# Attention scores of two heads: the products with the keys' low halves on 64 rows each, one head in the lower rows of TensorE, the other in the upper

## The chip, the cores and the metric

The kernel runs on one core of a Trainium2 chip, in one launch. The metric is device time in microseconds (us) from start to end of one execution; the median of several executions is compared. TensorE (PE) multiplies matrices, with its loads of the stationary operand shown apart (PEld); VectorE is DVE, ScalarE is ACT, GpSimd is POOL, and SyncE (SP) issues the transfers.

## What is computed

Two layers of a backbone over 512 latent tokens with a prefix of 256 context tokens, width 1024. Each layer projects its normed input once (`w_in`) to all branches: multi-scale pooling, windowed attention (8 query heads, 2 key/value heads, window of 128, all of the context, a sink per head) and differential attention (4 heads, each with two sets of scores over all 768 keys). The branches are gated, merged, and followed by a squared-ReLU MLP. The second layer needs no output for the context. What the change touches are the scores of the latent queries:

```python
s_loc = jnp.einsum('bnqhgd,bnkhd->bnhgqk', qb, kb, preferred_element_type=jnp.float32) * scale
s_ctx = jnp.einsum('bnqhgd,bkhd->bnhgqk', qb, k_ctx, preferred_element_type=jnp.float32) * scale
...
s1 = jnp.einsum('bqhd,bkhd->bhqk', q1, k1, preferred_element_type=jnp.float32) * scale
s2 = jnp.einsum('bqhd,bkhd->bhqk', q2, k2, preferred_element_type=jnp.float32) * scale
```

The head dimension is 64, half of TensorE's 128 rows.

## The kernel before

**Two halves.** Products run in float32r, a float32 of fewer bits. So that little is lost, each operand is split: a high half (rounded by ACT) and a low half (what is left, subtracted by DVE). A general product takes three matmuls: high by high, low by high, high by low. Each matmul has its own weight load.

**Scores.** With a head dimension of 64 the two halves of a query stand in one operand. `proj_tr` (L485) transposes the rotated queries of two heads into one PSUM tile and writes `Q`, 128 rows by head pair, head and 128 queries: for head 0 the high half lies in rows 0 to 63 and the low half in rows 64 to 127, for head 1 the other way round. The keys are transposed twice, so that rows 64 to 127 repeat rows 0 to 63, and split into `KH` and `KL`. One matmul of `Q` with `KH` over 128 rows so gives (high + low of the query) by the key's high half, and one of `Q` with `KL` adds the part with the key's low half, into the same PSUM tile `S`, two banks of 512 columns; there are two such tiles.

**Units.** A unit is 128 queries by two heads. `diff_unit` (differential, 16 units in each layer) takes 768 keys in pieces of 512 and 256 columns (L533, L534). `swa_unit` (windowed, 16 units in each layer) takes for the first and the last block of queries two pieces of 256, for the two in the middle pieces of 128, 384 and 128 (L698, L699). The stages of a unit are A (scores, row minimum on DVE at L535 or L700, exponential on ACT at L537 or L704), B (scaling), B2 (transposes `ptr` on PE, L557 or L737), C (product with the values), D. `diff_ctx` and `swa_ctx` handle context queries in the first layer and aren't changed.

**Order.** `attention` runs the units as a pipeline of steps: in each, B2 of the unit before, A of this one, and between them the projection of the next head group (`z`, L398) in two halves, its rotation and transposes, C and D of earlier units, and whole gate products (`gate`, L1016 to L1018) that have nothing to do with the scores. A scheduler then fixes each engine's order from priorities. PE executes in that fixed order.

After attention come the merge (`br`), `out` and the MLP (`ff`), nearly all matmuls of 256 or 512 columns.

Of the kernel before, what the change touches and what calls it, by code (L numbers as in the profile page):

```python
# [134 lines left out]
class Kern:  # L135
# [377 lines left out]
            d["Q"][t] = q  # L513


    def diff_unit(self, l, d, qt):
        nc = self.nc
        mm = nc.tensor.matmul
        KH, KL, V, hd = d["KH"], d["KL"], d["V"], d["gi"]
        u = {}  # L520
        kts = list(range(6)) if qt < 4 else [4, 5]
        ka = kts[0] * 128
        n = 768 - ka
        nk = len(kts)

        def A():
            q = d["Q"].pop(qt)
            u["nm"], u["r"], u["E"] = self.sm(2, "nm"), self.sm(2, "r"), []
            nm, r = u["nm"], u["r"]
            for i in range(2):  # L530
                S = self.s("S")
                for (c0, c1) in ((ka, 512), (512, 768)) if qt < 4 else ((512, 768),):
                    mm(S[:, c0 - ka:c1 - ka], q[:, 0, i, :], KH[:, i, c0:c1], start=True, stop=False)  # L533
                    mm(S[:, c0 - ka:c1 - ka], q[:, 0, i, :], KL[:, i, c0:c1], start=False, stop=True)  # L534
                nc.vector.tensor_reduce(nm[:, i:i + 1], S[:, 0:n], axis=AX.X, op=ALU.min)  # L535
                e = self.ap.tile([128, NT], F32, tag="E", name="E")
                nc.scalar.activation(e[:, 0:n], S[:, 0:n], AF.Exp, bias=nm[:, i:i + 1], scale=-1.0,  # L537
                                     accum_out=r[:, i:i + 1])
                u["E"].append(e)

        def B():
            E, r = u["E"], u["r"]
            rc = u["rc"] = self.sm(2, "rc")
            nc.vector.reciprocal(rc, r)
            c2 = self.sm(1, "c2")
            nc.vector.tensor_scalar(c2, rc[:, 1:2], r[:, 0:1], self.nlam[:, l:l + 1], ALU.mult, ALU.mult)
            nc.vector.scalar_tensor_tensor(E[0][:, 0:n], E[1][:, 0:n], c2, E[0][:, 0:n], ALU.mult, ALU.add)

        def B2():
            E = u["E"]  # L550
            u["PT"] = []
            trs = []
            for j0 in range(0, nk, 3):
                j1 = min(nk, j0 + 3)
                tr = self.g("ptr")
                for j in range(j0, j1):
                    nc.tensor.transpose(tr[:, (j - j0) * 128:(j - j0 + 1) * 128], E[0][:, j * 128:(j + 1) * 128],  # L557
                                        self.ident)
                trs.append((tr, j1 - j0))
            for tr, w in trs:  # L560
                PT = self.ap.tile([128, 2, 4, 128], F32R, tag="PT", name="PT")
                src = tr[:, 0:w * 128].rearrange("p (j d) -> p j d", d=128)
                nc.scalar.activation(PT[:, 0, 0:w, :], src, AF.Copy)
                nc.vector.tensor_tensor(PT[:, 1, 0:w, :], src, PT[:, 0, 0:w, :].bitcast(F32), op=ALU.subtract)
                u["PT"].append(PT)

        def C():
            rc = u["rc"]
            O = self.g("O")
            for j, kt in enumerate(kts):  # L570
                pt = u["PT"][j // 3]
                mm(O[:, 0:256], pt[:, 0, j % 3, :], V[:, kt, :], start=j == 0, stop=False)
                mm(O[:, 0:128], pt[:, 1, j % 3, :], V[:, kt, 0:128], start=False, stop=j == nk - 1)
            ob = u["ob"] = self.st("ob")
            nc.scalar.activation(ob[:, 0:128], O[:, 128:256], AF.Copy, scale=rc[:, 0:1])
            nc.vector.scalar_tensor_tensor(ob[:, 128:256], O[:, 0:128], rc[:, 0:1], ob[:, 0:128], ALU.mult, ALU.add)  # L576
            ssq = self.sm(1, "ssq")
            nc.scalar.activation(ob[:, 256:384], ob[:, 128:256], AF.Square, accum_out=ssq)
            u["rs"] = self.sm(1, "rso")
            self.rsqrt(u["rs"], ssq, 1, 1.0 / 128)  # L580

        def D():
            ob = u["ob"]
            nc.vector.tensor_scalar(ob[:, 0:128], ob[:, 128:256], u["rs"], None, ALU.mult)
            yt = self.g("yt")
            nc.tensor.transpose(yt[:, 0:128], u["ob"][:, 0:128], self.ident)
            y = self.ap.tile([128, 2, 128], F32, tag="y", name="y")
            nc.scalar.activation(y[:, 0, :], yt[:, 0:128], AF.Copy, scale=self.subln[:, l:l + 1])
            nc.sync.dma_start(self.yd[1][hd][:, qt * 128:(qt + 1) * 128], y[:, 0, :])

        return A, B, B2, C, D

    def diff_ctx(self, l, d):
# [6 lines left out]
        def A():  # L600
            nm, r = u["nm"], u["r"] = self.sm(4, "nm"), self.sm(4, "r")
            S = self.s("S")
            for j in range(2):
                q = d["Q"].pop(4 + j)
                for i in range(2):
                    o = (2 * j + i) * 256
                    mm(S[:, o:o + 256], q[:, 0, i, :], KH[:, i, 512:768], start=True, stop=False)
                    mm(S[:, o:o + 256], q[:, 0, i, :], KL[:, i, 512:768], start=False, stop=True)
# [62 lines left out]
    def swa_unit(self, l, d, qt, hp):  # L671
        nc = self.nc
        mm = nc.tensor.matmul
        KH, KL, V, g = d["KH"], d["KL"], d["V"], d["gi"]
        u = {}
        if qt >= 4:
            pieces, kts, m0 = [(0, 512, 256)], [4, 5], 0
        elif qt == 0:
            pieces, kts, m0 = [(0, 0, 256), (256, 512, 256)], [0, 1, 4, 5], 3
        elif qt == 3:  # L680
            pieces, kts, m0 = [(0, 512, 256), (256, 256, 256)], [4, 5, 2, 3], 0
        else:
            pieces = [(0, 512, 128), (128, (qt - 1) * 128, 384), (512, 640, 128)]
# [6 lines left out]
        def A():  # L690
            q = d["Q"][qt]
            if hp == 1:
                d["Q"].pop(qt)
            nm, r, E = u["nm"], u["r"], u["E"] = self.sm(2, "nm"), self.sm(2, "r"), []
            for i in range(2):
                S = self.s("S")
                for (o, c, w) in pieces:
                    mm(S[:, o:o + w], q[:, hp, i, :], KH[:, 0, c:c + w], start=True, stop=False)  # L698
                    mm(S[:, o:o + w], q[:, hp, i, :], KL[:, 0, c:c + w], start=False, stop=True)  # L699
                nc.vector.tensor_tensor_reduce(  # L700
                    S[:, 0:n], S[:, 0:n], self.mask[:, m0 * 128:m0 * 128 + n], 1.0, nsk[:, i:i + 1],
                    ALU.add, ALU.min, nm[:, i:i + 1])
                e = self.ap.tile([128, NT], F32, tag="E", name="E")
                nc.scalar.activation(e[:, 0:n], S[:, 0:n], AF.Exp, bias=nm[:, i:i + 1], scale=-1.0,  # L704
                                     accum_out=r[:, i:i + 1])
                E.append(e)
            dd = self.sm(2, "d")
            nc.vector.tensor_tensor(dd, nm, nsk, op=ALU.subtract)
            es = u["es"] = self.sm(2, "es")
            nc.scalar.activation(es, dd, AF.Exp)  # L710
# [34 lines left out]
        def C():  # L745
# [10 lines left out]
            for i in range(2):  # L756
                nc.sync.dma_start(
                    self.yd[0][2 * g + hp][i * 64:(i + 1) * 64, qt * 128:(qt + 1) * 128], y[0:64, i, :])

        return A, B, B2, C, lambda: None  # L760

    def swa_ctx(self, l, d, qt):
# [799 lines left out]
```

## Time and profile before

| | |
|---|---|
| time, 3 runs | 2240.76 us median (2237.43 to 2241.3) |
| profiled execution | 2242.5 us, its span 2240.4 us |
| PE busy | 2188.2 us, 98% of the span, 12924 matmuls |
| weight loads (PEld) busy | 1952.9 us, 87% |
| DVE, ACT, POOL busy | 1501.9, 961.6, 232.2 us |
| granted TensorE clock, mean | 0.996 of 2.4 GHz |

A matmul's busy time runs until its last result is out, so two that follow each other overlap in the record; how far apart they start says what one costs. In a row, "128\*128" behind MATMUL or LDWEIGHTS is the part of the array that is used, rows by columns, and "128x512" what streams through it.

### The profile page before, as it was taken

The page shows a single profiled execution, that of the slowest core. Times are in us where ns is not written, and L with a number is a line of the kernel's source. Part 1 is how long each engine was busy: PE and PEld are TensorE (multiplying, and loading weights), DVE is VectorE, ACT ScalarE, POOL GpSimd, SP SyncE. Part 2 cuts the span into 40 slices and gives each one's busy share as a digit, 9 for nine tenths or more (in the row PEclk, how much of TensorE's full clock was granted, in tenths as well). Part 3 has the DMA queues.
Part 4 walks back from the last instruction along what each step waited for, and adds up shares of the span by engine and source line. Part 5 has one row for each costly group of instructions (what it writes and reads, how often), then busy time and mean ns, then how long its engine had stood idle before and what let it go on. Part 6 is the DMA issues. An engine that isn't in the chain of part 4 may idle for free.

```text
span 2240.4 us, 34089 instructions
## 1 busy us (share of the span) xinstructions
PE 2188.2 (98%) x12924; PEld 1952.9 (87%) x12924; DVE 1501.9 (67%) x2883; ACT 961.6 (43%) x1981; POOL 232.2 (10%) x353
## 2 busy tenths in 40 slices
PE   7999999989999999999999989999999999999999
PEld 3899999988888888888888879999998889888887
DVE  5887667787696787655554487776778677444443
ACT  4456665565323432212222255665556435322331
POOL 3222122230000000000000002122221000000000
PEclk9999999999999999999999999999999999999999
DMA  6432122212874344333333342313222754333332
GB/s 253 144 98 79 55 82 71 74 44 65 271 237 169 116 156 152 130 129 120 129 118 103 99 129 75 94 46 86 75 72 83 237 184 135 101 97 98 93 99 71
DMA packets 108954, 261.58 MB, mean 117 GB/s; under 512 B 13043, under 2 KB 33651, under 8 KB 107510
## 3 DMA queue, kind: packets, MB, share of 16 engines
q1 hardware_dynamic: 108790, 259.40, 36.4%
q8 instruction: 102, 1.67, 0.3%
q14 instruction: 62, 0.51, 0.1%
HBM read 234.05 MB, written 25.30 MB: 116 GB/s over the span
## 4 chain that ended last, share of the span: by engine, by line
PE 65%; DVE 7%; DMA 3%; ACT 2%; issue 2%; POOL 1%; SPq 0%; POOLq 0%; ACTq 0%; DVEq 0%
PE ff L231 13%; PE ff L230 13%; PE ff L232 13%; PE z L398 4%; PE br L231 2%; PE br L232 2%; PE br L230 2%; DMA raw<-in_w_dram 2%; PE gate L1016 2%; PE gate L1018 2%; PE gate L1017 2%; DVE W L172 1%; PE out L232 1%; PE out L231 1%; PE out L230 1%
## 5 line engine op out<-in xcount | busy, mean ns | idle before, releaser
L171 ACT ACTIVATE W<-raw 128x768 fp32r<-128x768 f32 (+1 forms) x383 | 320.7, 839 | 595.3 <-PE ff L232 427.2
L172 DVE TENSOR_TENSOR W<-raw,W 128x768 fp32r<-128x768 f32 (+2 forms) x379 | 360.8, 954 | 231.4 <-ACT W L171 226.6
L398 PE MATMUL z<-W,h 128*128 128x384 f32 (+2 forms) x1728 | 314.1, 332 | 8.7 <-ACT h L1100 2.9
L398 PEld LDWEIGHTS z<-W,h 128*128 128x128 f32 x1728 | 287.1, 191 | 13.4 <-ACT h L1100 3.2
L231 PE MATMUL ff<-h,W 128*128 128x512 f32 (+1 forms) x800 | 280.8, 351 | 0.0
L230 PE MATMUL ff<-h,W 128*128 128x512 f32 (+1 forms) x800 | 280.6, 351 | 0.0
L232 PE MATMUL ff<-h,W 128*128 128x512 f32 (+1 forms) x800 | 280.5, 351 | 0.0
L231 PE MATMUL ff<-f,W 128*128 128x512 f32 x736 | 264.5, 359 | 0.1
L230 PE MATMUL ff<-f,W 128*128 128x512 f32 x736 | 263.6, 358 | 0.0
L232 PE MATMUL ff<-f,W 128*128 128x512 f32 x736 | 262.7, 357 | 0.0
L179 POOL TENSOR_TENSOR rs<-ms,mhalf 128x4 f32<-128x4 f32 (+4 forms) x79 | 82.7, 1047 | 1313.6 <-DVE ms L178 1239.0
L1016 PE MATMUL gate<-h,W 128*128 128x256 f32 (+1 forms) x656 | 213.2, 325 | 1.8 <-DVE ob L576 1.8
L1017 PE MATMUL gate<-h,W 128*128 128x256 f32 (+1 forms) x656 | 213.4, 325 | 0.0
L1018 PE MATMUL gate<-h,W 128*128 128x256 f32 (+1 forms) x656 | 210.5, 321 | 0.0
L1407 DVE SCALAR_TENSOR_TENSOR x<-ff,mod,x 128x512 f32<-128x512 f32 (+1 forms) x192 | 121.5, 658 | 103.8 <-PE ff L232 103.6
L278 DVE CUSTOM_DVE_ANT_0 junk<-wada,cbc,cols 128x1024 bf16<-128x1024 f32 x112 | 143.4, 1280 | 47.8 <-DMA wada<-in_wada_dram 47.4
L230 PEld LDWEIGHTS ff<-h,W 128*128 128x128 f32 x800 | 151.4, 189 | 21.4
L232 PEld LDWEIGHTS ff<-h,W 128*128 128x128 f32 x800 | 151.2, 189 | 21.5
L231 PEld LDWEIGHTS ff<-h,W 128*128 128x128 f32 x800 | 151.2, 189 | 21.4
L230 PEld LDWEIGHTS ff<-f,W 128*128 128x128 f32 x736 | 138.8, 189 | 21.5
L232 PEld LDWEIGHTS ff<-f,W 128*128 128x128 f32 x736 | 138.4, 188 | 21.3
L231 PEld LDWEIGHTS ff<-f,W 128*128 128x128 f32 x736 | 138.8, 189 | 20.8 <-DVE f L1381 0.5
(262 smaller groups left out, 4444.5 us busy)
## 6 DMA issues: line engine op xcount, KB each, us to landing
raw<-in_w_dram SPq DMA_DIRECT2D x375, 384.0 KB, 3.1
wada<-in_wada_dram SPq DMA_DIRECT2D x80, 512.0 KB, 4.1
wa<-in_wada_dram SPq DMA_DIRECT2D x8, 1024.0 KB, 8.1
tgd<-tgs SPq DMA_DIRECT2D x38, 192.0 KB, 1.9
tgl<-tgd SPq DMA_DIRECT2D x19, 384.0 KB, 4.9
tgd<-tgs SPq DMA_DIRECT2D x44, 128.0 KB, 1.7
tgl<-tgd SPq DMA_DIRECT2D x22, 256.0 KB, 3.8
yl<-yd SPq DMA_DIRECT2D x12, 384.0 KB, 4.8
```

The costliest lines, as they stand in the source:

```text
L171: nc.scalar.activation(H, src, AF.Copy)
L172: (eng or nc.vector).tensor_tensor(L, src, H.bitcast(F32), op=ALU.subtract)
L179: nc.gpsimd.tensor_tensor(out, t, self.mhalf[:, 0:n], op=ALU.pow)
L230: mm(ps[:, a:b], wh, x[0][:, r], start=k == 0, stop=False)
L231: mm(ps[:, a:b], wh, x[1][:, r], start=False, stop=False)
L232: self.last_mm = mm(ps[:, a:b], wl, x[0][:, r], start=False, stop=k == nk - 1)
L278: self.nc.vector.tensor_tensor_reduce(junk, w, c[:, v, :], 0.5, self.col(l, 21 + j), ALU.mult, ALU.add, self.mod[l][:, v, j:j + 1])
L398: self.nc.tensor.matmul(z[:, c0:384], h[k][:, hpart, ts], d["W"][k // 2][:, wpart, (k % 2) * 384 + c0:(k % 2 + 1) * 384], start=(k == 0 an ...
L1016: mm(ps, wh, x[:, 0, a:b], start=k == 0, stop=False)
L1017: mm(ps, wh, x[:, 1, a:b], start=False, stop=False)
L1018: return mm(ps, wl, x[:, 0, a:b], start=False, stop=k == len(acts) - 1)
L1407: nc.vector.scalar_tensor_tensor(x[m][:, ga:gb], ps[:, ga:gb], self.mod[l][:, v, 40 + m:41 + m], x[m][:, ga:gb], ALU.mult, ALU.add)
```

## The change

`diff_unit` and `swa_unit` no longer compute the scores head by head. A new function `scores` takes both `S` tiles at once and goes through the pieces: for each piece first both heads' products with `KH`, over 128 rows as before, then both heads' products with `KL`, each over 64 rows only, those in which the high half of that head's query lies: rows 0 to 63 for head 0 and rows 64 to 127 for head 1. The product of the query's low half with the key's low half is thereby left out. The number of matmuls and of weight loads stays the same; 288 of them (2 for each of 144 pieces) are now matmuls over a 64-row part of the array, at row 0 or at row 64.

```diff
+    def scores(self, q, k, pieces):
+        mm = self.nc.tensor.matmul
+        SS = [self.s("S") for _ in range(2)]
+        for (o, c, w) in pieces:
+            for i in range(2):
+                mm(SS[i][:, o:o + w], q[:, i, :], k(i, c, c + w)[0], start=True, stop=False)
+            for i in range(2):
+                p = slice(64 * i, 64 * i + 64)
+                mm(SS[i][:, o:o + w], q[p, i, :], k(i, c, c + w)[1][p], start=False, stop=True)
+        return SS
...
+            SS = self.scores(q[:, 0], lambda i, c0, c1: (KH[:, i, c0:c1], KL[:, i, c0:c1]),
+                             [(c0 - ka, c0, c1 - c0) for c0, c1 in (((ka, 512), (512, 768)) if qt < 4 else ((512, 768),))])
             for i in range(2):
-                S = self.s("S")
-                for (c0, c1) in ((ka, 512), (512, 768)) if qt < 4 else ((512, 768),):
-                    mm(S[:, c0 - ka:c1 - ka], q[:, 0, i, :], KH[:, i, c0:c1], start=True, stop=False)
-                    mm(S[:, c0 - ka:c1 - ka], q[:, 0, i, :], KL[:, i, c0:c1], start=False, stop=True)
+                S = SS[i]
                 nc.vector.tensor_reduce(nm[:, i:i + 1], S[:, 0:n], axis=AX.X, op=ALU.min)
...
+            SS = self.scores(q[:, hp], lambda i, c0, c1: (KH[:, 0, c0:c1], KL[:, 0, c0:c1]), pieces)
             for i in range(2):
-                S = self.s("S")
-                for (o, c, w) in pieces:
-                    mm(S[:, o:o + w], q[:, hp, i, :], KH[:, 0, c:c + w], start=True, stop=False)
-                    mm(S[:, o:o + w], q[:, hp, i, :], KL[:, 0, c:c + w], start=False, stop=True)
+                S = SS[i]
                 nc.vector.tensor_tensor_reduce(
```

On PE, a unit of differential attention in the first layer, between the last gate product and the next projection, stood like this before (S are the scores, one row for each matmul; "x3" means three that read alike):

```order
L1018 MATMUL gate<-h_170,W_3704 128x384
L533 MATMUL S<-KH,Q 128x512
L534 MATMUL S<-KL,Q 128x512
L533 MATMUL S<-KH,Q 128x256
L534 MATMUL S<-KL,Q 128x256
L533 MATMUL S<-KH,Q 128x512
L534 MATMUL S<-KL,Q 128x512
L533 MATMUL S<-KH,Q 128x256
L534 MATMUL S<-KL,Q 128x256
L398 MATMUL z<-W_3601,h_163 128x384 x3
```

The same place on PE of the changed kernel, whose L526 is the product over 64 rows:

```order
L1029 MATMUL gate<-h_170,W_3704 128x384
L523 MATMUL S<-KH,Q 128x512 x2
L526 MATMUL S<-KL,Q 128x512 x2
L523 MATMUL S<-KH,Q 128x256 x2
L526 MATMUL S<-KL,Q 128x256 x2
L398 MATMUL z<-W_3601,h_163 128x384 x3
```

The work around it stays where it was; the two heads are interleaved, and a unit of two pieces now goes from 128-row to 64-row matmuls and back twice. A unit of windowed attention with three pieces, on PE in the first layer, stood so before (its first head, with transposes of the unit before mixed in):

```order
L737 MATMUL ptr<-ident,E 128x128 x2
L698 MATMUL S<-KK,Q 128x128
L699 MATMUL S<-KK,Q 128x128
L737 MATMUL ptr<-ident,E 128x128
L698 MATMUL S<-KK,Q 128x384
L737 MATMUL ptr<-ident,E 128x128
L699 MATMUL S<-KK,Q 128x384
L698 MATMUL S<-KK,Q 128x128
L699 MATMUL S<-KK,Q 128x128
```

The same place on PE of the changed kernel, with both heads:

```order
L748 MATMUL ptr<-ident,E 128x128 x2
L523 MATMUL S<-KK,Q 128x128 x2
L748 MATMUL ptr<-ident,E 128x128
L526 MATMUL S<-KK,Q 128x128 x2
L748 MATMUL ptr<-ident,E 128x128
L523 MATMUL S<-KK,Q 128x384 x2
L526 MATMUL S<-KK,Q 128x384 x2
L523 MATMUL S<-KK,Q 128x128 x2
L526 MATMUL S<-KK,Q 128x128 x2
```

Here there are three goes to 64 rows and back, and the transposes, which use all 128 rows, never stand between the two heads' products over 64 rows. Over the whole program the changed kernel has 150 stretches of 64-row matmuls on PE, 138 of them a pair and 12 a single matmul (six pairs near the end of attention, four of 512 and two of 256 columns, were pulled apart), so 300 changes of shape; all other matmuls of PE keep their order but for three moves by a few places, and POOL's order is the same. On DVE the row minimum of the first head now stands some places later, behind pieces of work that stood between the two heads before.

## Rows read from the trace of the kernel before

**Rows 1.** The page's first part: the span, and TensorE's busy time.

```profile
span 2240.4 us, 34089 instructions
PE 2188.2 (98%) x12924; PEld 1952.9 (87%) x12924; DVE 1501.9 (67%) x2883; ACT 961.6 (43%) x1981; POOL 232.2 (10%) x353
```

**Rows 2.** Busy time by stretch, the attention of both layers, with granted clock.

```profile
95.00:330.00 235.00, 230.82 (x1498) 225.15 (x1497) 177.80 (x437) 143.84 (x360) 48.34 (x64) 1.00 0.28 84
330.00:520.00 190.00, 183.21 (x1154) 174.04 (x1154) 143.85 (x348) 112.92 (x312) 54.02 (x93) 1.00 0.19 58
1300.00:1420.00 120.00, 112.11 (x817) 109.16 (x815) 93.64 (x233) 67.15 (x158) 21.44 (x28) 0.97 0.28 83
1420.00:1730.00 310.00, 304.74 (x2250) 295.19 (x2249) 229.77 (x552) 188.74 (x476) 69.24 (x121) 1.00 0.28 80
```

**Rows 3.** Timeline of PE in a unit of differential attention: start, duration, instruction.

```profile
325.10 0.34 PE L1017 MATMUL gate<-h,W 128*128 128x384 f32 x1
325.27 0.34 PE L1018 MATMUL gate<-h,W 128*128 128x384 f32 x1
325.44 0.39 PE L533 MATMUL S<-KH,Q 128*128 128x512 f32 x1
325.67 0.40 PE L534 MATMUL S<-KL,Q 128*128 128x512 f32 x1
325.91 0.28 PE L533 MATMUL S<-KH,Q 128*128 128x256 f32 x1
326.02 0.28 PE L534 MATMUL S<-KL,Q 128*128 128x256 f32 x1
326.14 0.40 PE L533 MATMUL S<-KH,Q 128*128 128x512 f32 x1
...
326.71 0.29 PE L534 MATMUL S<-KL,Q 128*128 128x256 f32 x1
```

**Rows 4.** Timeline of the weight loads, in that unit.

```profile
325.45 0.19 PEld L534 LDWEIGHTS S<-KL,Q 128*128 128x128 f32 x1
```

**Rows 5.** Timeline of the weight loads, in a windowed unit with pieces of 128.

```profile
1503.47 0.19 PEld L699 LDWEIGHTS S<-KK,Q 128*128 128x128 f32 x1
1503.58 0.19 PEld L698 LDWEIGHTS S<-KK,Q 128*128 128x128 f32 x1
1503.69 0.19 PEld L699 LDWEIGHTS S<-KK,Q 128*128 128x128 f32 x1
```

**Rows 6.** Timeline of PE in the prologue, the first change of shape.

```profile
12.37 1.05 PE L1075 MATMUL ada<-wa,ccol 128*2 128x512 f32 x2
13.35 0.69 PE L1117 MATMUL rb<-row,ident 3*128 3x512 f32 x1
```

**Rows 7.** Timeline of PE and PEld in the prologue, a change to 128 rows by 128.

```profile
42.59 0.59 PE L1075 MATMUL ada<-wa,ccol 128*2 128x512 f32 x1
43.12 0.45 PE L398 MATMUL z<-W,h 128*128 128x384 f32 x1
43.12 0.30 PEld L398 LDWEIGHTS z<-W,h 128*128 128x128 f32 x2 [0.86 <-issue]
```

**Rows 8.** Timeline of PE in the prologue, the last change of shape.

```profile
46.78 0.40 PE L1086 MATMUL adat<-ident,arow 2*128 2x2 f32 x4
47.11 0.44 PE L398 MATMUL z<-W,h 128*128 128x384 f32 x1
```

**Rows 9.** PE's waits, first layer's attention, last row second's: us, times, longest.

```profile
PE tr L495 <- DVE rot L484: 2.9, 2, 1.7
PE tr L495 <- DVE rc L620: 2.2, 1, 2.2
PE ptr L737 <- DVE E L724: 1.9, 1, 1.9
PE ptr L557 <- DVE E L547: 1.3, 3, 0.6
```

**Rows 10.** Row minimum and exponential of differential units: busy, mean ns.

```profile
L535 DVE TENSOR_REDUCE nm<-S 128x1 f32<-128x768 f32 x64 | 58.4, 950 | 0.8 <-PE S L534 0.5
L537 ACT ACTIVATE E<-S,nm 128x768 f32<-128x768 f32 x64 | 57.2, 899 | 46.3 <-DVE nm L535 46.2
```

## The prediction

> **What bounds the kernel now.** I read the page's busy times first: PE is busy for 2188.2 of 2240.4 us and DVE, the next, for 1501.9 [rows 1], so time that PE gains or loses should mostly reach the end. That share is a mean, so next come the stretches of attention, the only ones that the change touches: over the two layers PE is busy for 830.9 of 855 us, DVE for 645.1, at the full clock of 2.4 GHz nearly throughout (1.00, once 0.97) [rows 2]. Only 24.1 us of PE's time there are open. So the question is what the scores cost PE in sequence, which the timeline tells by how far apart matmuls start.
>
> In a differential unit the products start 0.23 us apart where 512 columns stream and 0.115 apart where 256 do; 384 columns take 0.17 [rows 3]. That is 0.45 ns a column, with the weight load hidden: it starts 0.01 us after the matmul before it (load at 325.45, matmul at 325.44) [rows 3, 4], so it runs while that one streams. With 128 columns (0.058 us of streaming) the loads, 0.11 us apart, set the pace [rows 5]. A matmul's result is out some 0.165 us after its last column (0.34 us recorded against 0.17 from start to start) [rows 3].
>
> **What a change of shape costs.** The change brings something that attention does not have now: matmuls over 64 rows between matmuls over 128. Before, PE changes the part of the array that it uses 14 times, all in the prologue, the first at 13.35 and the last at 47.11 us [rows 6, 8]. There the next load does not start with the matmul before it: at the first, the matmul before ends at 12.37 + 1.05 = 13.42 and the next shape begins at 13.35, 0.07 before that end [rows 6]; 43.12 against 42.59 + 0.59 = 43.18 [rows 7]; 47.11 against 46.78 + 0.40 = 47.18 [rows 8]. It is so in 13 of the 14 (in the other the next one waited for ACT anyway). The load so isn't brought forward: it waits until the results are nearly out, 0.165 − 0.07 = 0.095 us after the last column, and then takes the 0.11 us of a load [rows 5], in the open. Sum 0.20 us from last column to first column. The first matmul after a change confirms it: it is recorded at 0.45 and 0.44 us in place of 0.34, so its columns began 0.11 and 0.10 later than its start, at 43.23 and 47.21 [rows 3, 7, 8]; the columns of the one before ended 0.165 before its end, at 43.015 and 47.015; the gaps are 0.215 and 0.195. I take **0.20 us**. None of the 14 is between 128 and 64 rows; they are between 128, 32 rows and 32 columns, and two kinds agree, so I carry the number over.
>
> **The change part by part.** Changes of shape: 150 stretches of 64-row matmuls, entered and left, are 300 × 0.20 = **+60.0 us**.
>
> Saved columns: if the two 64-row matmuls of a pair stream at the same time, a piece streams three times its width in place of four. By piece, from the code's loops: 32 of 512 columns save 0.23 each, 7.4; 64 of 256 save 0.115, 7.4; 16 of 384 save 0.17, 2.8. The 32 of 128 took four loads, 0.44 us; now two loads lie inside the changes already counted, and 0.11 + 2 × 0.058 = 0.226 is left, a saving of 0.21, in all 6.8. Sum **−24.4 us**. Six pairs are pulled apart and lose this: four of 512, two of 256, **+1.2**.
>
> Second load of a pair: after a change two loads follow each other by 0.11 us (two took 0.30 where one takes 0.19) [rows 7]. If the upper head's load comes after the lower head's, its matmul trails by that: 138 × 0.11 = **+15.2 us**. If the two loads run together, nothing. If the matmuls themselves don't overlap, the second streams its whole width behind the first, and in place of 15.2 it is 28 × 0.23 + 62 × 0.115 + 16 × 0.17 + 32 × 0.11 = 19.8. So PE's sequence grows by 36.8 (loads together), 52.0 (loads in turn) or 56.6 us (nothing together). The row nearest to it has loads in turn, so I take **52.0**.
>
> On loading in turn a page differs from this row. The Trainium skill, "TensorEngine Tiling (Array Packing)", Key Properties, says that different tiles can load and multiply in parallel; the rows show loads in turn only for one and the same part of the array, so they cannot refute it. By the page the sum would be 36.8, by the row 52.0.
>
> Waits: of the 24.1 us open in attention some are for chains that don't hang on the scores, such as rotated keys (2.9, 2.2) [rows 9]. More PE work ahead of them shortens them; I put 8 us on it, of at most 24.1. Against that, head 0's scores are complete later: its last product started at 326.02, head 1's at 326.71 [rows 3], and now both end together, so DVE's first minimum (0.95 us) starts some 0.7 us later and the second queues behind it [rows 10]. What waits for that are the next step's transposes of E; they wait little now, 1.9 us at one place in the first layer and 1.3 at three in the second [rows 9], since a step's projection and gate products lie between. I put 3 us on it (a fifth of 64 units late by a quarter of a microsecond), and at most 9 (a quarter of them by 0.55). Net **−5**, between −24 and +9 at the outermost, between −11 and +6 as I would have it. DVE, ACT, POOL and SP get no new work; the same weights stream, later by what PE lost, and after attention nothing changes.
>
> **Sum.** 60.0 − 24.4 + 1.2 + 15.2 − 5 = **+47 us**. The profiled execution took 2242.5 us, 0.1% over the median of the runs, 2240.8; on the median that gives 2287.8, so **2288 us**.
>
> **Rivals.**
>
> *Loads together.* The sum is 36.8 − 5 = +32, 2273 us. What speaks for it is that the two loads go to different rows; against it, that all rows have loads in turn. Chance 0.27.
>
> *The pairs don't run side by side*, so the change doesn't do what it says. 56.6 − 5 = +52, 2292 us. The rows show no two matmuls at the same time, and the new code does not order the two otherwise than any others. Chance 0.17.
>
> *Faster: no change of shape between 128 and 64 rows is paid.* It could be that a load for half of the rows goes ahead as any other. Then, with loads in turn, each piece costs its columns or four loads of 0.11, whichever is more: 512 saves 0.23 (28 times, 6.4), 384 saves 0.17 (16 times, 2.8), 256 saves 0.02 (62 times, 1.2), 128 nothing: −10, 2230 us; with loads together −20 (28 × 0.23 + 62 × 0.115 + 16 × 0.17 + 32 × 0.11), 2221 us. The point from which it decides: with loads in turn the change pays if a change of shape costs under (24.4 − 1.2 − 15.2) / 300 = 0.027 us, with loads together under 0.077; the rows have 0.20. The Trainium skill, "TensorE: Matmul & The Clock Gate", Part 3, has four matmuls of 32 rows run 3.07 times as fast as in turn, and counts no price for going in and out of the packing; no run here shows that, and the 13 rows with a wait for the end speak against leaving the price out. Chance 0.08.
>
> *Hidden.* The open 24.1 us of PE take up nearly all of a small sum (loads together, all waits gone): 36.8 − 24.1 = +13 at best, so no change within 0.2% (4.5 us, about what a measurement of this kernel can tell from none) needs a cheaper change of shape too, of some 0.14 us or less. Chance 0.02.
>
> *Late scores.* If the transposes of E waited after most units, 64 × 0.55 = 35 more, so 2320 us. The step's other work speaks against it. Chance 0.03.
>
> **How the numbers follow.** My forecast, with loads in turn and pairs side by side, has 0.43; the time is its time. Slower by over 0.2% are it and the rivals of loads together, pairs not side by side and late scores: 0.43 + 0.27 + 0.17 + 0.03 = 0.90. Faster 0.08, same 0.02. The range leaves the faster and the late cases out: from loads together with the waits at their better bound, 36.8 − 11 = +26, 2266, to nothing together with waits at the worse, 56.6 + 6 = +63, 2304.
>
> **What would show it.** At each go from `KH` to `KL` products the first load of a 64-row matmul should start 0.07 us before the end of the matmul before it and not with its start; the same when leaving. The two 64-row matmuls of a pair should start 0.11 us apart and the pair of 512 columns take 0.34 us from first column to last, not 0.46. PE's attention should be longer by some 25 us in each layer, and merge, `out` and MLP as long as before. The prediction is wrong if 64-row loads start with the 128-row matmul before them (then it is faster), if a change costs much else than 0.20 us, or if PE's waits for E grow past 9 us.

## The result, and the profile after

The changed kernel takes 2275.99 us (median of four executions, 2275.26 to 2277.36) against 2241.03 (four, 2237.43 to 2244.01): 35 us slower. The ratio is 1.0142, 95% interval 1.0119 to 1.0165. The forecast was 2288 us in a range of 2266 to 2304, slower with a chance of 0.90.

The page's first lines for the changed kernel answer to [rows 1]:

```profile
span 2274.2 us, 34079 instructions
PE 2223.9 (98%) x12924; PEld 1944.1 (85%) x12924; DVE 1504.2 (66%) x2883; ACT 960.7 (42%) x1981; POOL 238.5 (10%) x353
```

The span grew by 33.8 us and PE's busy time by 35.7, so PE's open time shrank by 1.9 us, from 52.2 to 50.3. DVE, ACT and POOL did the same work as before. By the busy times per stretch (PE, PEld, DVE, ACT, POOL, granted clock, transfers) PE is as full in attention as it was in [rows 2], and nearly always at the upper of its two clock levels:

```profile
95.00:330.00 235.00, 231.41 (x1453) 216.24 (x1452) 172.47 (x425) 139.21 (x350) 47.66 (x61) 1.00 0.26 82
330.00:545.00 215.00, 208.88 (x1259) 186.79 (x1258) 157.45 (x376) 122.91 (x334) 58.70 (x102) 0.99 0.18 56
1420.00:1760.00 340.00, 334.81 (x2383) 306.34 (x2383) 242.23 (x583) 199.03 (x503) 76.79 (x126) 1.00 0.25 74
```

The first of these stretches has 1453 matmuls in the 235 us that held 1498 before [rows 2]: the same engine, just as busy by the record, gets less done. The timeline of PE and PEld in the same differential unit as [rows 3] shows why (start, duration, instruction; x2 are the two heads):

```profile
333.57 0.34 PE L1029 MATMUL gate<-h,W 128*128 128x384 f32 x1
333.75 0.63 PE L523 MATMUL S<-KH,Q 128*128 128x512 f32 x2
334.30 0.50 PE L526 MATMUL S<-KL,Q 64*128 64x512 f32 x2
334.73 0.50 PE L523 MATMUL S<-KH,Q 128*128 128x256 f32 x2
335.16 0.38 PE L526 MATMUL S<-KL,Q 64*128 64x256 f32 x2
335.48 0.79 PE L398 MATMUL z<-W,h 128*128 128x384 f32 x3
...
334.30 0.18 PEld L526 LDWEIGHTS S<-KL,Q 64*128 64x128 f32 x2 [0.36 <-issue]
334.73 0.30 PEld L523 LDWEIGHTS S<-KH,Q 128*128 128x128 f32 x2 [0.24 <-issue]
335.16 0.19 PEld L526 LDWEIGHTS S<-KL,Q 64*128 64x128 f32 x2
```

Three things are to be seen. First, at each change of shape the next load starts 0.06 to 0.08 us before the end of the matmuls before it, as these rounded rows have it: 334.30 against 333.75 + 0.63 = 334.38, 334.73 against 334.80, 335.16 against 335.23, 335.48 against 335.54. (In the trace the median of all 300 changes is 0.072.) Second, the two 64-row loads take 0.18 us together, as long as one, and the two matmuls 0.50 us together: both heads run side by side from the first column. Third, the price: from the load of the 512-column pair to the load of the next shape there are 0.43 us, of which 0.23 are columns; for the 256-column pair 0.32, of which 0.115 are columns. The rest, 0.20 us, is one change of shape; it rests on starts of loads alone, while the ends of matmuls are modelled in the profile. Reckoned as in the prediction, from the last column to the first of the next shape, the median of the 300 is 0.20 us too. Two changes and one pair of 512 cost 0.63 us where two whole products cost 0.46 before.

From the first projection (`z`) to the first merge product (`br`) PE takes 570.0 and 454.8 us in the two layers, against 552.5 and 438.6 before: 17.5 and 16.2 us longer, where the forecast had some 25 each. The rest of the program is as long as it was.

### The profile page after: what moved, and what is told of

The parts are those of the page before. It is cut to its first block, busy times and chain, and to the rows that moved or that the text cites. A ratio compares the mean times of both kernels' runs of the same rounds, so it can differ in the third digit from the quotient of the medians.

```text
span 2274.2 us, 34079 instructions
## 1 busy us (share of the span) xinstructions
PE 2223.9 (98%) x12924; PEld 1944.1 (85%) x12924; DVE 1504.2 (66%) x2883; ACT 960.7 (42%) x1981; POOL 238.5 (10%) x353
## 4 chain that ended last, share of the span: by engine, by line
PE 82%; DVE 9%; DMA 4%; ACT 2%; issue 2%; POOL 1%; SPq 0%; POOLq 0%; ACTq 0%; DVEq 0%
PE ff L231 13%; PE ff L230 13%; PE ff L232 13%; PE z L398 9%; PE gate L1027 4%; PE gate L1029 4%; PE gate L1028 4%; PE S L523 2%; PE br L231 2%; PE S L526 2%; PE br L232 2%; PE br L230 2%; DMA raw<-in_w_dram 2%; DVE W L172 1%; PE ptr L748 1%
```

## The experiments

Ten runs followed, on three chips, of eight other kernels and of the changed kernel itself. Each stands against the kernel before on the same chip, and all ratios are to that. The edits are shown against the changed kernel.

**Interleaved, but over all 128 rows.** What does the order alone do?

```diff
-                p = slice(64 * i, 64 * i + 64)
-                mm(SS[i][:, o:o + w], q[p, i, :], k(i, c, c + w)[1][p], start=False, stop=True)
+                mm(SS[i][:, o:o + w], q[:, i, :], k(i, c, c + w)[1], start=False, stop=True)
```

> The order of the changed kernel (per piece both heads' KH products, then both heads' KL products), but the KL products over all 128 rows, so no change of shape in attention. Theory 1 (the loss is 300 changes of shape at 0.20 us, less the columns that the pairs save): the same PE work as before, so 2241 us within 5. Rival (the loss comes from the interleaving: head 0's scores are complete later, and the transposes of E and the scores' row minima wait): most of the 35 us stay, 2265 to 2276 us.

Measured: 2259.54 us, ratio 1.0059 (1.0040 to 1.0077). My theory had it as before; it lost 13 us with no change of shape in attention. The rival, that most of the 35 us would stay, fell too. So the order has a price of its own. (Order means that of all engines: this kernel executes the same order as the changed one on PE, DVE, ACT and POOL, and on DVE it differs from that of before at 154 of 2883 places.)

**All KH products of a unit, then all its pairs in one stretch.**

```diff
...
         for (o, c, w) in pieces:
             for i in range(2):
-                mm(SS[i][:, o:o + w], q[:, i, :], k(i, c, c + w)[0], start=True, stop=False)
+                mm(SS[i][:, o:o + w], q[:, i, :], k(i, c, c + w)[0], start=o % 512 == 0, stop=False)
+        for (o, c, w) in pieces:
             for i in range(2):
                 p = slice(64 * i, 64 * i + 64)
...
```

> All KH products of a unit first, then all its pairs of 64-row KL products in one stretch: 136 changes of shape in place of 300, the same pairs. Theory 1: 136 x 0.20 = 27 us for changes; a differential unit takes four KH products (0.69 us), two changes (0.40) and 0.345 of pairs, 1.435 against 1.38 before; a windowed one of two pieces 1.09 against 0.92; one of three 1.48 against 1.58; in all +3 us on before, +4 with the four stretches that the order breaks: 2245 us, 31 less than the changed kernel. Rival (a 64-row matmul or its pairing is dear in itself, whatever the changes): as many 64-row matmuls, so the time stays near 2276.

Measured: 2260.02 us, ratio 1.0055 (1.0033 to 1.0076), so 16 to 20 us less than the changed kernel, not 31. PE's busy time was right within 3.4 us: 2195.6, 7.4 over before, where 4 were expected. But PE's open time grew from 52.2 to 56.7 us (span 2252.3), and the median lay another 6 us over this profiled execution (2254.12). The changes of shape cost about what they should; the open time is new beside the changed kernel, which has 50.3 us of it. Why the other executions took 6 us more than the profiled one is not shown.

**Both heads' KL products in the same rows.**

```diff
-                p = slice(64 * i, 64 * i + 64)
+                p = slice(0, 64)
```

> As the changed kernel with its 300 changes, but both heads' KL products stand in rows 0 to 63, so that none can run beside the other; for head 1 the rows then hold the query's low half, so the product with its high half is left out and another takes its place. Theory 1 with pairs that truly run side by side: the second product of each pair adds its width, 28 x 0.23 + 62 x 0.115 + 16 x 0.17 + 32 x 0.11 = 20 us, 2296 us. Rival (side by side gives nothing, the record only shows them so): 2276 us.

Measured: 2298.08 us, ratio 1.0230 (1.0207 to 1.0253). The span is 2293.2 us, 19.0 over the changed kernel's, where 20 were expected. The unit shown above, on PE and PEld of this kernel:

```profile
340.57 0.73 PE L526 MATMUL S<-KL,Q 64*128 64x512 f32 x2
341.23 0.50 PE L523 MATMUL S<-KH,Q 128*128 128x256 f32 x2
...
340.57 0.29 PEld L526 LDWEIGHTS S<-KL,Q 64*128 64x128 f32 x2 [0.36 <-issue]
```

Two loads now take 0.29 us, so the second starts 0.11 after the first, and the pair takes 0.73 in place of 0.50: in turn. Side by side is real, and it needs different rows.

**Each KL product alone.**

```diff
         for (o, c, w) in pieces:
             for i in range(2):
                 mm(SS[i][:, o:o + w], q[:, i, :], k(i, c, c + w)[0], start=True, stop=False)
-            for i in range(2):
                 p = slice(64 * i, 64 * i + 64)
```

> The 64-row KL product follows its head's KH product at once, so each stands alone: 574 changes of shape and nothing side by side. Theory 1: 574 x 0.20 = 115 us, less some 7 for loads of the 128-column pieces that now lie inside changes: about 2348 us. Rival (a change costs little and the loss is elsewhere): it loses only the pairing, 20 us on the changed kernel, 2296 us.

Measured: 2357.76 us, ratio 1.0498 (1.0476 to 1.0520), 111 us over before where 107 were expected. That the sums agree so well is in part luck: the mean granted clock is 0.986 here against 0.994 or 0.995 in most runs of before, which by an estimate (0.009 of 2355 us) is up to some 20 us that the expectation had no term for. The price of a change is better read from the starts. At the 566 of its 574 changes where the clock was at its upper level, the median from last column to first is 0.20 us again.

**No KL products.**

```diff
-                mm(SS[i][:, o:o + w], q[:, i, :], k(i, c, c + w)[0], start=True, stop=False)
-            for i in range(2):
-                p = slice(64 * i, 64 * i + 64)
-                mm(SS[i][:, o:o + w], q[p, i, :], k(i, c, c + w)[1][p], start=False, stop=True)
+                mm(SS[i][:, o:o + w], q[:, i, :], k(i, c, c + w)[0], start=True, stop=True)
```

> Both heads' KH products per piece, interleaved, and no KL products at all (the part of the scores with the keys' low halves is left out): what those products cost in the kernel before, so the most that any form of them can give back. By columns and loads: 64 x 0.23 + 128 x 0.115 + 32 x 0.17 + 64 x 0.11 = 42 us less PE work than before, 2199 us on a before of 2241, if all of it reaches the end. Rival from the run with the products interleaved over 128 rows, which lost 13 us with no change of shape: the same waits come back, or more of them, since less PE work covers them, 2212 us or over.

Measured, in one execution: 2218.32 us, 26 under the 2244.15 of before. PE's busy time is 2154.5 us of a span of 2216.5: 33.7 less than before, while the open time grew from 52.2 to 62.0. The rival was right: in this order, leaving the KL products out altogether gives back only 1.2%. No run leaves them out head by head, without the price of the interleaved order.

**Head by head in the new function.** Is it the interleaving or the place of the minima in the code?

```diff
-        for (o, c, w) in pieces:
-            for i in range(2):
-                mm(SS[i][:, o:o + w], q[:, i, :], k(i, c, c + w)[0], start=True, stop=False)
-            for i in range(2):
-                p = slice(64 * i, 64 * i + 64)
-                mm(SS[i][:, o:o + w], q[p, i, :], k(i, c, c + w)[1][p], start=False, stop=True)
+        for i in range(2):
+            for (o, c, w) in pieces:
+                kh, kl = k(i, c, c + w)
+                mm(SS[i][:, o:o + w], q[:, i, :], kh, start=True, stop=False)
+                mm(SS[i][:, o:o + w], q[:, i, :], kl, start=False, stop=True)
```

> The new function, but its products head by head over all 128 rows: PE's order is that of before, and only DVE's and ACT's orders differ by a few places, since both heads' minima come behind all products in the code. If the interleaving of the two heads' products is what cost 13 us in the run without changes of shape, this one is as before, within 0.2%. Rival: the 13 us came from the place of the minima in the code, or from taking both score tiles at once; then this one has them too, +0.6%.

Measured: 2246.05 us, ratio 1.0000 (0.9982 to 1.0018). PE's order is exactly that of before, and DVE's differs at 16 places. The code around the products costs nothing that this run can tell.

**The changed kernel again.**

> The changed kernel itself, unaltered, beside these runs on one chip, so that the others can be set against it there: 1.4 to 1.6% over before.

Measured: 2276.78 us, ratio 1.0135 (1.0104 to 1.0165), a little less than expected, and within the interval of the first.

**One stretch, only in the windowed units of three pieces.** These are the units in which the pairs should save more than two changes cost. In short:

```diff
+        if len(pieces) == 3:
+            ...
+            return SS
+        for i, (o, c, w) in [(i, x) for i in range(2) for x in pieces]:
+            kh, kl = k(i, c, c + w)
+            mm(SS[i][:, o:o + w], q[:, i, :], kh, start=True, stop=False)
+            mm(SS[i][:, o:o + w], q[:, i, :], kl, start=False, stop=True)
```

> Pairs over 64 rows only in the 16 windowed units of three pieces, each unit's KH products first and its three pairs in one stretch; every other unit head by head over 128 rows, in the order of before. 32 changes of shape, 6 us, against the loads and columns saved, 16 x 0.5. Theory 1: PE's work falls by 16 x 0.10 = 1.6 us; the interleaving of a quarter of the units may give back up to 3 us of waits; so within 0.2% of before. Rival (a stretch costs more than its two changes): slower by over 0.2%.

Measured: 2246.68 us, ratio 1.0008 (0.9996 to 1.0020). No gain, and no sign that a stretch costs more than its changes: the interval ends at the 0.2% that the rival asked for.

**Head 1's products first.** Nothing is interleaved. The edit is shown against the head-by-head run above.

```diff
-        for i in range(2):
+        for i in (1, 0):
             for (o, c, w) in pieces:
                 kh, kl = k(i, c, c + w)
```

> Head by head over all 128 rows, as before, but head 1's products ahead of head 0's; nothing is interleaved and no shape changes. On DVE the minimum of head 0 stays ahead of that of head 1 in the windowed units that were looked at with pieces of 128, and in the differential units it is the scheduler's choice, head 1's first in those looked at. If what cost 13 us in the interleaved run over 128 rows is that the scores that DVE takes first are complete later, this one loses part of it: some 6 us, 0.3%. If it is the interleaving in itself on PE, it is as before.

Measured: 2263.11 us, ratio 1.0073 (1.0058 to 1.0089), 19 us where I expected some 6. So an order of the heads can cost as much without any interleaving. But the reason that I gave, scores that are complete later than DVE wants them, is mostly not what the trace shows: in 23 of the 32 differential units DVE's first minimum starts within 0.2 us of where it did before, counted from the unit's first product. Here is one differential unit of the second layer, before and then in this run:

```profile
1595.88 1.81 DVE L535 TENSOR_REDUCE nm<-S 128x1 f32<-128x768 f32 x2
1596.87 0.91 ACT L537 ACTIVATE E<-S,nm 128x768 f32<-128x768 f32 x1 [2.00 <-DVE nm L535]
...
1609.98 1.82 DVE L547 TENSOR_REDUCE nm<-S 128x1 f32<-128x768 f32 x2
1611.83 0.90 ACT L549 ACTIVATE E<-S,nm 128x768 f32<-128x768 f32 x1 [3.52 <-DVE nm L547]
```

Before, ACT's first exponential starts when the first of the two row minima is done; now it starts when both are (1609.98 + 1.82 = 1611.80). It is so in 43 of the 64 units of latent queries, against none before and none head by head. That fits an order in which DVE takes head 1's minimum first, which is ready first, while ACT still takes head 0's exponential first. So what is late here is the chain behind the scores, and by this reading it is ACT's order that makes it late.

**The interleaved run over 128 rows again**, on that chip.

> The run with the products interleaved over 128 rows once more, beside the one with head 1 first on one chip: 0.4 to 0.8% over before again, if that loss is one of the order and not of the chip.

Measured: 2255.50 us, ratio 1.0052 (1.0039 to 1.0065). The loss belongs to the order, not to a chip. Some of PE's waits over the whole run (us in total, times, longest), first before:

```profile
PE tr L495 <- DVE rot L484: 4.4, 4, 1.7
PE ptr L737 <- DVE E L724: 1.9, 1, 1.9
PE gate L1016 <- DVE ob L576: 1.8, 3, 0.6
PE ptr L557 <- DVE E L547: 1.7, 4, 0.6
```

In this interleaved run:

```profile
PE gate L1026 <- DVE ob L588: 5.3, 4, 1.9
PE tr L495 <- DVE rot L484: 5.2, 4, 1.5
PE ptr L569 <- DVE E L559: 3.5, 8, 0.6
PE ptr L747 <- DVE E L734: 2.2, 2, 1.8
```

And in the changed kernel:

```profile
PE tr L495 <- DVE rot L484: 4.7, 4, 1.5
PE gate L1027 <- DVE ob L589: 2.0, 3, 0.7
PE ptr L748 <- DVE E L735: 1.7, 1, 1.7
PE ptr L570 <- DVE E L560: 1.0, 2, 0.5
```

The interleaved run has the transposes of E wait at 8 places in differential units, and gate products wait longer for `ob`, DVE's result of stage C; the changed kernel is back near the kernel before in both. How close this comes can be read in the second layer, where fewer gate products and no context queries lie between. In the head-by-head run, whose PE order is that of before, DVE ends the scaling of E at 1566.29 + 1.02 = 1567.31, and the first transpose's load follows 0.88 us later:

```profile
1566.29 1.02 DVE L559 SCALAR_TENSOR_TENSOR E<-E,c 128x768 f32<-128x768 f32 x1
1568.19 0.14 PEld L569 LDWEIGHTS ptr<-ident,E 128*128 128x128 f32 x1
```

In the interleaved run, same place, E is ready at 1569.07 and the transpose, which has waited for it, follows at once:

```profile
1568.05 1.02 DVE L559 SCALAR_TENSOR_TENSOR E<-E,c 128x768 f32<-128x768 f32 x1
1569.18 0.14 PEld L569 LDWEIGHTS ptr<-ident,E 128*128 128x128 f32 x1 [0.67 <-ACT y L600]
1569.21 0.30 PE L569 MATMUL ptr<-ident,E 128*128 128x128 f32 x1 [0.50 <-DVE E L559]
```

Read in this way for all 32 differential units (from the end of E's scaling to the next load of a transpose of E), the median margin is 1.70 us before, 1.68 head by head, 0.37 interleaved over 128 rows, 0.88 in the changed kernel and 2.22 with each KL product alone. With one stretch a unit it is 0.48, with head 1 first 0.33.

Later scores are only a part of what makes the chain late in the interleaved kernels. This is the unit shown above for head 1 first, in the interleaved run:

```profile
1600.07 0.63 PE L523 MATMUL S<-KH,Q 128*128 128x512 f32 x2
1601.23 0.40 PE L525 MATMUL S<-KL,Q 128*128 128x256 f32 x2
1603.14 0.29 DVE L483 TENSOR_TENSOR rot<-rg,t 128x128 f32<-128x128 f32 x1 [0.77 <-POOL t L461]
1603.69 1.81 DVE L547 TENSOR_REDUCE nm<-S 128x1 f32<-128x768 f32 x2
```

All scores are complete at 1601.23 + 0.40 = 1601.63, but DVE takes the rotation `rot` first, and for that it stands idle for `t` from POOL. The first minimum starts 2.06 us after the scores are complete. Before, the minima came ahead of `rot` here. With the interleaving `rot` stands right ahead of the minima in 6 of the 32 differential units, before in none. In 13 of the 32 the first minimum starts over 1.2 us later than before, counted from the unit's first product, and that is more than the 0.6 us by which head 0's scores are later.

## Why the prediction was right, and where it was off

**Direction and range** held, by the step that I gave as the main one: a change of shape between 128 and 64 rows costs 0.20 us, carried over from changes of another kind in the prologue [rows 6 to 8]. It is shown by the timeline above, by the same 0.20 us at the changes of the kernel that has 574, and by PE's busy time in the kernel with 136. That the range held says less than it seems to: it was wide enough for the rivals on loads and pairs as well.

**The columns saved** were sized right. The pairs run side by side, and without that the kernel is 19 us slower (20 in the forecast).

**The second load of a pair, +15.2 us, was wrong.** It is nothing: loads for different rows start together, and the first rival, "loads together" (2273 us, chance 0.27), was the one that came. I took the value of the nearest row, [rows 7], but that row shows two loads for the same rows. The kernel with both products in the same rows has just that 0.11 us. With the term at 0 the sum for PE is 36.8 us, and PE's busy time grew by 35.7. So the 12 us by which the forecast lay too high are this term, less 3 us from the waits. The Trainium skill, "TensorEngine Tiling (Array Packing)", Key Properties, has tiles load and multiply in parallel; the traces agree, 0.18 us for two loads in different rows against 0.29 in the same.

**The waits, −5 us,** were −1.9. The net was small as forecast, but what lies behind it was not. I had the late scores delay DVE's first minimum by some 0.7 us and priced that at 3 us, at most 9. I left out that the scheduler would give DVE another order as well, although it stands with the change that the first minimum moves behind other pieces of work. In the kernels interleaved over 128 rows the whole order costs 0.5 to 0.6%, 11 to 13 us. Of the 12.3 us that the second one's span (2252.7) is over [rows 1], PE's open time, 61.1 us with 2191.6 busy, accounts for 8.9. The other 3.4 are busy time. The trace has PE at the lower clock level for 23.9 us in place of 17.1, which at half the speed costs (23.9 − 17.1) / 2 = 3.4 us, an estimate from the two levels. In the first interleaved run the mean granted clock was 0.991 to 0.993, against 0.994 or 0.995 in most runs of before, so by an estimate (0.002 of 2250 us) some 4 or 5 of its 13 us can be clock.

In the changed kernel the price of the order hardly shows. It executes the same order as the interleaved kernel, but 300 changes of shape make each step longer on PE, and the late chain on DVE and ACT has that much more time: the margin is 0.88 us and not 0.37, and PE's open time 50.3 us and not 61.1. So the price of the change covers the price of its order. The kernel with one stretch a unit fits in between (margin 0.48, open time 56.7). With fewer changes part of the waits came back. Of the 9.1 us by which its span fell short of the expected gain of 31 (2252.3 against 2274.2), 6.4 are PE's open time and 2.7 its busy time.

What the runs show is that a late chain from the scores to the transposes and products behind them goes with the loss. The margin is 1.70 and 1.68 us in the two kernels that are fast, 0.37 and 0.33 in the two that lose 11 to 19 us with no change of shape. What makes the chain late is the order, and not of PE alone: scores that are complete later, `rot` ahead of the minima on DVE, and with head 1 first the order on ACT. How much of the loss is due to each stays open, since no run interleaves PE's products and keeps DVE's and ACT's order. Nor is it only the transposes of E that wait. With head 1 first they wait 1.8 us in differential units, as before, and the gate products wait 7.9 us for `ob`, against 1.8.

**Faster** was out of reach in this form: the pairs save 24 us of columns and loads, and even with one stretch a unit 136 changes cost 27. A unit would have to get by with fewer than two changes to keep more than a trace of it.

**A slip in the rival Hidden** changes nothing: with all of its 24.1 us gone, no change within 0.2% needs a change of shape of (24.4 − 1.2 + 24.1 + 4.5) / 300 = 0.17 us or less, not 0.14.

## What to carry to other kernels

Before packing small products beside each other, count how often TensorE must change the shape that it works in: each change opens a gap of 0.20 us here, as much as 440 columns, so a stretch between two changes must save that twice. Bring all products of the small shape into one stretch, and look whether their number pays at all: here even leaving them out gave only 1.2%, in the interleaved order. And when one engine's order changes, look at what a scheduler made of the others': here a minimum that moved behind `rot`, or an exponential that waited for the second head, went with a loss of 11 to 19 us. That a profile shows no new waits may only mean that the same change made their cover longer.

## What was not expected of the hardware

Where 64-row products alternate with 128-row ones one by one, TensorE's granted clock fell in attention although the record has no idle time. Busy time by stretch of the kernel with each KL product alone (PE, PEld, DVE, ACT, POOL, granted clock, transfers):

```profile
150.00:160.00 10.00, 10.00 (x56) 9.09 (x55) 4.74 (x14) 3.75 (x9) 1.00 (x2) 0.92 0.09 27
160.00:165.00 5.00, 5.00 (x18) 4.41 (x18) 2.80 (x8) 1.78 (x5) 0.00 (x0) 0.69 0.02 3
165.00:175.00 10.00, 10.00 (x60) 8.64 (x58) 5.69 (x12) 6.44 (x14) 2.81 (x3) 0.98 0.22 66
175.00:180.00 5.00, 5.00 (x22) 4.86 (x22) 3.20 (x9) 2.61 (x6) 0.63 (x2) 0.66 0.25 79
```

Over that run the clock was 0.986 of 2.4 GHz in the mean, against 0.996 before: for parts of these stretches it was at the lower level, 1.2 GHz, with PE recorded as busy throughout. A busy share of 100% in the record says nothing of the gaps inside, at changes of shape, since a matmul's busy time runs on into them. Whether the gaps or the 64 rows brought the clock down is not shown; the changed kernel, with 300 changes, stayed at 0.995.
